# Feed-forward weights of blocks 3 to 14 loaded in pairs into the three buffers that later hold activations

## The chip, the core and the metric

The kernel runs on one core of a Trainium2 chip. The core has five engines with queues of their own: TensorE (PE, matrix products; its weight loads are shown as PEld), VectorE (DVE), ScalarE (ACT), GpSimd (POOL) and SyncE (SP). SP does no arithmetic here; it issues nearly all transfers between the chip's main memory (HBM) and the core's memory (SBUF). Each engine works through its own instructions in a fixed order and stops at one whose inputs or buffers are not ready; whatever stands behind it on that engine stops too. Matrix results land in PSUM, in banks that must be read out before they are used again.

The metric is device time in microseconds (us) of one execution.

## What is computed

One step of a model layer over 640 tokens (128 of a prompt, 512 of a sample) with a width of 1024: two mixers, an output projection with a layer norm, and then the feed-forward part, which is where the change lies. The last stage of the reference, cut to what matters:

```python
D_MODEL = 1024
D_FF = ((8 * D_MODEL // 3 + 255) // 256) * 256      # 2816

x = layer_norm(ALPHA * x + gate1 * mix, p['ln1_g'], p['ln1_b'])
h = x * (1.0 + scale2) + shift2
gt, up = jnp.split(h @ p['ffn_w_in'], 2, axis=-1)   # (1024, 2 * 2816)
ff = (jax.nn.silu(gt) * up) @ p['ffn_w_out']        # (2816, 1024)
x = layer_norm(ALPHA * x + gate2 * ff, p['ln2_g'], p['ln2_b'])
```

All of it is float32. The kernel gets float32 accuracy from a matrix unit that rounds its operands: it splits each operand into a high and a low part and sums three products (high x high, high x low, low x high).

## The kernel before

**Stages.** The program has a long first part (filters, the projections with `in_w_in`, the two mixers, `proj_a`, `proj_b`, `w_out`), up to about 970 us. Then comes the first half of the feed-forward part (`ffn_w_in`: gate and up projections, SiLU, product), up to 1267.8 us, and then the second half (`ffn_w_out`, the products named `fo`) to the end.

**The first half** walks over 22 blocks j of 128 feed-forward columns. Block 0 is done plainly. Blocks 1 to 21 use a Winograd-like scheme (class `Wino` with the name "f") that turns the gate and up products of a block into seven products of half the depth, numbered 1, 2, 4, 5, 6, 7 and 3; each is 12 matmuls of 128x320. Here `6_j` is short for product 6 of block j. They run into three PSUM banks per block (a: products 1, 6, 7, 4; b: 2; c: 5, 3), and after each product an ACT copy or a DVE operation (`post`, `ffn_done`) reads the bank before the next product adds to it. The tiles of these reads are `fc1`, `fu2`, `fu3` and `y`.

**Weights of a block.** Two loads of 512 KB, row 0 (gate columns, `rf0_j`) and row 1 (up columns, `rf1_j`), go into SBUF buffers with the tag "raw" (`Wino.raw`). There are `RAW_BUFS = 3` of these, so a block and a half. Then ACT rounds to the high part (`CAST`, names ending in h) and DVE subtracts for the low part (names ending in l): `wfg` from row 0 as loaded (products 1 and 2), `wfa` from half of row 1 (product 4), and, after three DVE additions and subtractions within the raw tiles, `wfs` (product 6), `wfu` (7 and 5), and after a fourth `wfv` (product 3). These split operands have 3 buffers (g, a, v) or 2 (s, u), so they can be made about two blocks before their products run. Both raw tiles of a block are free once its `wfu` and `wfv` parts are done. In the traces all these DVE operations stand under one line, that of the helper `tt`.

**What sets the order.** The program is written in periods (`PERIOD`): in period j stand the loads and splits of block j+1, then `6_j 2_j 1_(j+1) 4_(j-1) 5_j 7_j 3_(j-1)`. A scheduler then lays each engine's instructions out by its own estimate of when they can start, with priority for the bank reads. What it lays down is fixed; on the chip, an instruction that waits longer than estimated holds up its queue.

**Results.** The outputs of blocks 0 to 15 (`y_j`) are stored to HBM (`ad`), in the same SP queue as the loads. Those of blocks 16 to 21 stay in SBUF as `act8`, `act9` and `act10`: three buffers of 10,240 bytes per partition in the pool `arp`, opened at the end of `ffn_ops` and first written near 1210 us. The memory under this pool is that of the pool `lnr` (tiles `r` and `hf`, the normalised rows), which is closed just before, so that the first users of it wait for the last readers of `hf`.

Of the kernel before, what the change touches and what calls it, by code (L numbers as in the profile page):

```python
# [9 lines left out]
F32 = mybir.dt.float32  # L10
F32R = mybir.dt.float32r
# [6 lines left out]
P = 128  # L18
D = 1024
KT = 8  # L20
T = 640
# [109 lines left out]
FFN0 = "51 61 12 w2 71"  # L131
PERIOD = (("g", 1), ("w", 1), ("6", 0), ("2", 0), ("1", 1), ("4", -1), ("5", 0), ("7", 0), ("3", -1))
WPRI = 99
HIE = """SSSSVVSVSVSSSSSSSVVVSVVSVSSVSSSSSSSSSSSSSSSSSSSSSSSSSSSSSSSSSSSSSSSSSSSSSSSSSSSSSSSSSSSSSSSSSSSSSSSSSSSSSSSSSS"""
LOOK = """22222012202102201120122111222222222222222222222222222222222222222222222222222222222222222222222222222222222222"""
CONVSEQ = """a0 b0 c0 d0 e0 a1 b1 c1 f0 d1 e1 a2 b2 f1 s04 c2 s00 d2 x0 p0 s01 e2 i00 s02 a3 i01 s03 b3 i02 i03 f2 o00 c3 d3 e3 o01 a4 f3 s14 x1 s10 b4 c4 p1 s11 d4 i10 s12 e4 a5 i11 s13 b5 c5 d5 i12 f4 i13 o10 e5 a6 o11 f5 b6 s24 x2 s20 p2 s21 c6 i20 d6 s22 e6 i21 s23 a7 b7 i22 i23 c7 o20 f6 d7 o21 m0 e7 f7 s34 s30 n0 x3 m1 p3 s31 i30 s32 i31 s33 n1 i32 i33 o30 o31"""
# [26 lines left out]
def body(tc, I, O):  # L163
# [16 lines left out]
    def tt(out, a, b, op, eng=None):  # L180
        return (eng or V).tensor_tensor(out=out, in0=a, in1=b, op=op)  # L181
# [4 lines left out]
    def f32(ap):  # L186
        return ap.bitcast(F32)

    def pool(name, bufs=1, space=None, side=None):
        kw = dict(name=name, bufs=bufs, reuse_waits="tile")  # L190
        if space is not None:
            kw["space"] = space
        if side is not None:
            kw["side"] = side
        cm = tc.tile_pool(**kw)
        p = cm.__enter__()
        return p, (lambda: cm.__exit__(None, None, None))
# [6 lines left out]
    wp, close_wp = pool("wp")  # L204
# [132 lines left out]
    RAW_BUFS, HL_BUFS = 3, 3  # L337
    stream = dict(specs=[], hl=[], pos=0, stop=None)

    def w_fm(wap, col):  # L340
        return (wap.rearrange("(k p) n -> p k n", p=P)[:, :, col:col + P], (KT, P), None)
# [4 lines left out]
    def issue(i):  # L346
        src, (a, b), own = stream["specs"][i]
        raw = wp.tile([P, a, b], F32, tag="raw", bufs=RAW_BUFS, name=f"raw{i}")
        SY.dma_start(raw, src)
        if own is None:  # L350
            q, th, tl, n = wp, "wh", "wl", HL_BUFS
        else:
            q, th, tl, n = own[0]["p"], "wbh", "wbl", own[1]
        hi = q.tile([P, a, b], F32R, tag=th, bufs=n, name=f"wh{i}")
        lo = q.tile([P, a, b], F32R, tag=tl, bufs=n, name=f"wl{i}")
        with tc.high_priority():
            (V.tensor_copy if HIE[i] == "V" else S.copy)(hi, raw)  # L357
            tt(lo, raw, f32(hi), ALU.subtract, G if i < len(WSUB) and WSUB[i] == "G" else V)
        stream["hl"].append((hi, lo))
# [257 lines left out]
    def split(hl, at, src, eng="S"):  # L617
        h_, l_ = (x[(slice(None),) + at] for x in hl)
        (V.tensor_copy if eng == "V" else S.copy)(h_, src)
        tt(l_, src, f32(h_), ALU.subtract)  # L620


    class Wino:
# [5 lines left out]
            self.W, self.Y, self.B = {}, {}, {}  # L629

        def raw(self, j, row):
            t = wp.tile([P, KT, P], F32, tag="raw", bufs=RAW_BUFS, name=f"r{self.nm}{row}_{j}")
            SY.dma_start(t, w_fm(*self.cols(j)[row])[0])
            return t

# [887 lines left out]
    fn_ = {}  # L1523
# [52 lines left out]
    def plain_post(half):  # L1576
        g, u = (BK[x, half][:, 0:HT] for x in "gu")
        if half == 0:
            Y["y", 0] = fn_["p"].tile([P, T], F32, tag="y", bufs=3, name="y0")
            y = Y["y", 0][:, 0:HT]  # L1580
            act(y, g, AF.Silu)
            tt(y, u, y, ALU.mult)
        else:
            y1 = fn_["p"].tile([P, HT], F32, tag="u2", bufs=3, name="yp")
            act(y1, g, AF.Silu)
            half1(0, y1, u)

    def half1(j, y1, u):
        y = Y["y", j]
        tt(y[:, HT:HT + 64], y1[:, 256:HT], u[:, 256:HT], ALU.mult)  # L1590
        tt(y[:, HT + 64:T], y1[:, 0:256], u[:, 0:256], ALU.mult)
        if j < NSP:
            SY.dma_start(ad[j], y)
            return
        if j % 2 == 0:
            fn_["act", j // 2] = fn_["ar"].tile([P, 2, 2, T], F32R, name=f"act{j // 2}")
        t = fn_["act", j // 2]
        split((t[:, 0], t[:, 1]), (j % 2,), y)

# [6 lines left out]
    def ffn_done(n, j, ps):  # L1606
        Y = ffn.Y
        if n == 1:
            Y["c1", j] = ffn.keep("c1", 1, j, ps)
        elif n == 2:  # L1610
            Y["y", j] = fn_["p"].tile([P, T], F32, tag="y", bufs=3, name=f"y{j}")
            y = Y["y", j][:, 0:HT]
            tt(y, ps, Y["c1", j], ALU.add)
            act(y, y, AF.Silu)
        elif n == 6:
            Y["u2", j] = ffn.keep("u2", 3, j, ps)
        elif n == 7:
            u3 = ffn.keep("u3", 2, j, ps)
            tt(u3, ffn.B["c", j][:, 0:HT], u3, ALU.add)
            Y["u3", j] = u3  # L1620
        elif n == 4:
            y = Y["y", j][:, 0:HT]
            tt(y, ps, y, ALU.mult)
        elif n == 3:
            y1 = Y["u2", j]
            tt(y1, ps, y1, ALU.add)
            act(y1, y1, AF.Silu)
            half1(j, y1, Y["u3", j])

    ffn = Wino("f", lambda tag: fn_["p"], ffn_x, ffn_cols, ffn_done, WPRI)  # L1630
    W, Y, BK, ffn_run, prod_mm = ffn.W, ffn.Y, ffn.B, ffn.run, ffn.mm
# [154 lines left out]
```

## Time and profile before

| | us |
|---|---|
| median of 3 runs | 1429.8 (1427.77 to 1691.48) |
| the profiled execution | 1430.8 |
| its span in the profile | 1428.1 |
| first half of the feed-forward part, blocks 3 to 21 | about 1004 to 1267.8 |
| PE busy in the whole span | 1377.5 |

The span runs from the first to the last instruction; the 2.7 us between it and the execution's time lie around it. PE is busy nearly throughout, so what can be won is the time in which PE waits, and where matmuls follow one another closely a stretch is best read by their count: twelve back to back took 1.76 us. A row of the windows view gives, for a stretch of the span, its length, then the busy time of each engine with the count of instructions, the granted clock of PE, the busy share of the DMA engines and GB/s. In the rows of the timeline, what stands in brackets is the idle time of the engine before the row and what ended it.

### The profile page before, as it was taken

Reading aid. Unit: us, or ns where it says so; the run is one execution under the profiler, and the core shown is the slowest. Engines: PE = TensorE matmul, PEld = TensorE weight load, DVE = VectorE, ACT = ScalarE, POOL = GpSimd, SP = SyncE. Lnnn points to the kernel's source line nnn. Section 1 sums busy time; section 2 is a strip of 40 time slices with the busy share of each in tenths; the row PEclk is TensorE's granted clock in tenths of the full one; section 3 lists DMA queues with packets and bytes.
Section 4 is the critical chain, followed back from the end, with each engine's and each line's share of the span. In section 5 each row is a group of like instructions: output and inputs, shape, how many; then the busy total and the mean of one; then the engine's idle time right before and its main releaser. Section 6 shows DMA issues by size and latency. Waiting matters only on the chain. (4 is left out here: it accounts for less than half of the span.)

```text
span 1428.1 us, 23421 instructions
## 1 busy us (share of the span) xinstructions
PE 1377.5 (96%) x9513; PEld 1291.3 (90%) x9513; DVE 990.8 (69%) x1751; ACT 619.4 (43%) x1011; POOL 63.4 (4%) x56
## 2 busy tenths in 40 slices
PE   4989999999999999999999999998999999999997
PEld 2689889999999999999999999988999998998886
DVE  6886786647889734568778875578876766766427
ACT  3655554433323212455565673337444434442121
POOL 4230000020000000000000000000000000000003
PEclk9999999999999999999999999999999999999999
DMA  7944665674333374422232224632343233357211
GB/s 244 332 138 144 214 215 175 206 249 152 91 97 107 107 231 146 140 85 80 76 95 62 67 67 139 223 118 77 97 124 115 89 108 97 94 193 279 74 60 74
DMA packets 198855, 195.63 MB, mean 137 GB/s; under 512 B 7581, under 2 KB 155773, under 8 KB 197980
## 3 DMA queue, kind: packets, MB, share of 16 engines
q1 hardware_dynamic: 194860, 179.75, 40.0%
q0 software_dynamic: 2160, 9.15, 1.7%
q10 hardware_dynamic: 1728, 5.24, 0.9%
q8 instruction: 74, 1.21, 0.3%
q14 instruction: 33, 0.27, 0.1%
HBM read 162.91 MB, written 31.21 MB: 136 GB/s over the span
## 5 line engine op out<-in xcount | busy, mean ns | idle before, releaser
L181 DVE TENSOR_TENSOR wl<-raw,wh 128x1024 fp32r<-128x1024 f32 x96 | 117.2, 1223 | 134.1 <-ACT wh L357 133.4
L357 ACT CAST wh<-raw 128x1024 fp32r<-128x1024 f32 x90 | 94.1, 1049 | 221.1 <-PE pb L611 41.0
L1424 PE MATMUL fo<-wh,act 128*128 128x512 f32 (+1 forms) x440 | 130.6, 380 | 0.0
L1424 PEld LDWEIGHTS fo<-wh,act 128*128 128x128 f32 x440 | 81.2, 188 | 15.9
L1424 PE MATMUL fo<-wl,act 128*128 128x512 f32 (+1 forms) x220 | 83.4, 379 | 0.0
L611 PE MATMUL hy<-hTh,wh 128*128 128x320 f32 x256 | 79.6, 311 | 0.0
L611 PE MATMUL hy<-hTh,wl 128*128 128x320 f32 x256 | 79.1, 309 | 0.0
L611 PE MATMUL hy<-hTl,wh 128*128 128x320 f32 x256 | 79.1, 309 | 0.0
L611 PE MATMUL f<-hTh,wh 128*128 128x320 f32 x224 | 70.7, 316 | 0.0
L611 PE MATMUL f<-hTl,wh 128*128 128x320 f32 x224 | 69.6, 311 | 0.0
L611 PE MATMUL f<-hTh,wl 128*128 128x320 f32 x224 | 69.2, 309 | 0.0
L181 POOL TENSOR_TENSOR y<-y,gb 128x512 f32<-128x512 f32 x8 | 11.6, 1453 | 905.8 <-ACT y L170 905.5
L1424 PEld LDWEIGHTS fo<-wl,act 128*128 128x128 f32 x220 | 41.3, 188 | 7.9
L611 PEld LDWEIGHTS hy<-hTh,wh 128*128 128x128 f32 x256 | 48.1, 188 | 0.0
L611 PEld LDWEIGHTS hy<-hTl,wh 128*128 128x128 f32 x256 | 48.1, 188 | 0.0
L611 PEld LDWEIGHTS hy<-hTh,wl 128*128 128x128 f32 x256 | 48.0, 188 | 0.0
L170 ACT ACT_TABLE_LOAD x36 | 46.2, 1283 | 1.4 <-PEq L1770 0.7
L708 PE MATMUL v<-wh,hTl 128*128 128x256 f32 x160 | 45.1, 284 | 1.4 <-POOL hTl L181 1.4
L708 PE MATMUL v<-wl,hTh 128*128 128x256 f32 x160 | 44.8, 284 | 1.6 <-DVE wl L181 1.6
L708 PE MATMUL v<-wh,hTh 128*128 128x256 f32 x160 | 44.6, 283 | 0.0
L611 PEld LDWEIGHTS f<-hTl,wh 128*128 128x128 f32 x224 | 42.2, 188 | 0.0
L611 PEld LDWEIGHTS f<-hTh,wh 128*128 128x128 f32 x224 | 42.1, 188 | 0.0
(2291 smaller groups left out, 4699.1 us busy)
## 6 DMA issues: line engine op xcount, KB each, us to landing
raw<-in_w_in SPq DMA_DIRECT2D x52, 512.0 KB, 3.9
rf<-in_ffn_w_in SPq DMA_DIRECT2D x42, 512.0 KB, 4.9
araw<-in_ada_w SPq DMA_DIRECT2D x20, 1024.0 KB, 6.1
rm<-in_w_in SPq DMA_DIRECT2D x28, 512.0 KB, 4.8
raw<-in_ffn_w_out SPq DMA_DIRECT2D x22, 512.0 KB, 4.9
sd<-my SPq DMA_DIRECT2D x28, 320.0 KB, 2.3
kk<-kd SPq DMA_DIRECT2D x20, 256.0 KB, 2.6
ad<-y SPq DMA_DIRECT2D x16, 320.0 KB, 4.0
```

The costliest lines, as they stand in the source:

```text
L170: r = S.activation(out, in_, func, bias=bias, scale=scale)
L181: return (eng or V).tensor_tensor(out=out, in0=a, in1=b, op=op)
L357: (V.tensor_copy if HIE[i] == "V" else S.copy)(hi, raw)
L611: r = PE.matmul(ps[:, 0:HT], w[a][:, k, :], x[b][:, k, c0:c0 + HT], start=k == 0 and i == 0, stop=k == kt - 1 and i == 2)
L708: PE.matmul(ps[:, (t - t0) * 256:(t - t0) * 256 + 256], hT[b][:, k, t * P:t * P + P], w[a][:, k % 4, :], start=k == 0 and i == 0, stop=k = ...
L1424: PE.matmul(ps, x(t, b, k0 + kk), w[a][:, kk, :], start=first and kk == 0 and i == 0, stop=last and kk == nk - 1 and i == 2)
```

## The change

The raw weights of blocks 3 to 14 no longer go through the three "raw" buffers. Both rows of such a block go into one tile `rp{j}` of the pool `arp`, under the tag "act", which `act8` to `act10` now share. So there are three pair buffers for blocks 3 to 14 (twelve pairs, four turns), after which the same three buffers take the activations. The "raw" buffers, which blocks 3 to 14 leave alone, are next used by blocks 15 and up. The arithmetic is the same.

```diff
+FFN_PAIRS = range(3, 15)
...
         def raw(self, j, row):
-            t = wp.tile([P, KT, P], F32, tag="raw", bufs=RAW_BUFS, name=f"r{self.nm}{row}_{j}")
+            if self.nm == "f" and j in FFN_PAIRS:
+                if row == 0:
+                    pair = fn_["ar"].tile([P, 4 * T], F32, tag="act", bufs=3, name=f"rp{j}")
+                    self.W[j, "pair"] = pair[:, 0:2 * D].rearrange("p (r k n) -> p r k n", r=2, k=KT)
+                t = self.W[j, "pair"][:, row]
+            else:
+                t = wp.tile([P, KT, P], F32, tag="raw", bufs=RAW_BUFS, name=f"r{self.nm}{row}_{j}")
             SY.dma_start(t, w_fm(*self.cols(j)[row])[0])
             return t
...
-            fn_["act", j // 2] = fn_["ar"].tile([P, 2, 2, T], F32R, name=f"act{j // 2}")
+            fn_["act", j // 2] = fn_["ar"].tile([P, 2, 2, T], F32R, tag="act", bufs=3, name=f"act{j // 2}")
```

Since buffers come free at other times, the scheduler lays the instructions out differently from block 3 on. Three places show it. In each, `rf0_j` and `rf1_j` are the rows of block j in "raw" buffers and `rp{j}` is a pair (a load of it is one row of the pair).

SP's queue where block 3 begins, before:

```order
L1501 DMA xd_68<-r4_9803 128x1024
L633 DMA rf1_2_10604<-in_ffn_w_in 128x8x128
L633 DMA rf0_3_10641<-in_ffn_w_in 128x8x128
L1593 DMA ad_71<-y0_10438 128x640
L633 DMA rf1_3_10647<-in_ffn_w_in 128x8x128
L633 DMA rf0_4_10772<-in_ffn_w_in 128x8x128
L633 DMA rf1_4_10778<-in_ffn_w_in 128x8x128
L1593 DMA ad_71<-y1_10493 128x640
```

And in the changed kernel, at the same place:

```order
L1508 DMA xd_68<-r4_9803 128x1024
L640 DMA rf1_2_10604<-in_ffn_w_in 128x8x128
L640 DMA rf0_15_12201<-in_ffn_w_in 128x8x128
L1600 DMA ad_71<-y0_10438 128x640
L640 DMA rp3_10641<-in_ffn_w_in 128x8x128 x2
L640 DMA rp4_10771<-in_ffn_w_in 128x8x128 x2
L640 DMA rp5_10901<-in_ffn_w_in 128x8x128 x2
L640 DMA rf1_15_12207<-in_ffn_w_in 128x8x128
L640 DMA rf0_16_12332<-in_ffn_w_in 128x8x128
L1600 DMA ad_71<-y1_10493 128x640
```

Row 0 of block 15 takes the place of row 0 of block 3, three whole pairs follow the store of y0 together, and the rest of block 15 and a row of block 16 come right after them, about twelve blocks ahead of their use. The first row of `rp3` waits for the last reader of `hf`, the DVE operation `t4l<-hf1`.

ACT's queue where block 3 is split, before (`fc1`, `fu2`, `fu3` are the bank reads that PE's next products need):

```order
L677 COPY fu2_2_10681<-fa2_10589 128x320
L619 CAST wfa3h_10649<-rf1_3_10647 128x512
L619 CAST wfg4h_10774<-rf0_4_10772 128x1024
L677 COPY fu3_2_10752<-fa2_10589 128x320
L619 CAST wfs3h_10656<-rf0_3_10641 128x512
L619 CAST wfu3h_10660<-rf1_3_10647 128x1024
L619 CAST wfv3h_10665<-rf0_3_10641 128x512
```

And in the changed kernel:

```order
L620 CAST wfg3h_10643<-rp3_10641 128x1024
L620 CAST wfa3h_10648<-rp3_10641 128x512
L684 COPY fu2_2_10680<-fa2_10589 128x320
L620 CAST wfg4h_10773<-rp4_10771 128x1024
L620 CAST wfa4h_10778<-rp4_10771 128x512
L684 COPY fc1_3_10711<-fa3_10698 128x320
L620 CAST wfg5h_10903<-rp5_10901 128x1024
L620 CAST wfu3h_10659<-rp3_10641 128x1024
L684 COPY fu3_2_10751<-fa2_10589 128x320
L620 CAST wfs3h_10655<-rp3_10641 128x512
```

Casts of blocks 4 and 5 moved ahead of the cast `wfs3h`, which the first product of period 3 needs.

ACT's queue in a period in the middle, before (block 13 is split here; `fc1_12` reads product 1 of block 12, `fu3_11` product 7 of block 11):

```order
L170 ACTIVATE y11_11875<-y11_11875 128x320
L677 COPY fc1_12_11891<-fa12_11878 128x320
L619 CAST wfa13h_11959<-rf1_13_11957 128x512
L619 CAST wfg14h_12084<-rf0_14_12082 128x1024
L619 CAST wfu13h_11970<-rf1_13_11957 128x1024
L677 COPY fu3_11_11931<-fa11_11747 128x320
L619 CAST wfs13h_11966<-rf0_13_11951 128x512
L619 CAST wfv13h_11975<-rf0_13_11951 128x512
```

And in the changed kernel, at the same bank reads:

```order
L620 CAST wfg14h_12073<-rp14_12071 128x1024
L171 ACTIVATE y11_11865<-y11_11865 128x320
L684 COPY fc1_12_11881<-fa12_11868 128x320
L620 CAST wfa13h_11948<-rp13_11941 128x512
L620 CAST wfs13h_11955<-rp13_11941 128x512
L684 COPY fu3_11_11921<-fa11_11738 128x320
L620 CAST wfu13h_11959<-rp13_11941 128x1024
L620 CAST wfv13h_11964<-rp13_11941 128x512
```

Between `fc1_12` and the bank read `fu3_11` there stood three casts, of row 1 of block 13 and of row 0 of block 14, all from "raw" buffers; now two stand there, and `wfg14h` and `wfu13h` have moved to places ahead of `fc1_12` and behind `fu3_11`. All of them read pairs. From the split of block 16 on, each queue stands as it did before. SP then issues the store of y11, row 1 of block 16, the store of y12, row 0 of block 17, row 1 of block 17, and so on.

## The prediction

> **What bounds the kernel now.** I read the busy shares and the chain of waits first:
>
> ```profile
> PE 1377.5 (96%) x9513; PEld 1291.3 (90%) x9513; DVE 990.8 (69%) x1751; ACT 619.4 (43%) x1011; POOL 63.4 (4%) x56
> PE fo L1424 10%; DMA rf<-in_ffn_w_in 6%; PE pa L611 4%; PE wo L1424 4%; DVE rf L181 2%; PE fa L668 1%; PE mga L611 1%; PE fc L668 1%; DVE fu L181 1%; DVE y L181 1%; PE fg L1573 1%; PE fo_last L1424 1%; PE fb L668 0%; PE fu L1573 0%; DMA raw<-in_ffn_w_out 0%
> ```
>
> PE is at 96%, so at most some 50 us can be won anywhere. The chain's largest part that isn't PE is the load that the change moves, 6% of 1428, about 86 us. That isn't the gain: PE works beside it. What PE loses is read from the stage. The windows, cut where product 4 of blocks 3, 8 and 19 begins:
>
> ```profile
> 1035.90:1097.40 61.50, 61.50 (x422) 61.50 (x421) 45.59 (x74) 28.36 (x50) 0.00 (x0) 1.00 0.38 115
> 1097.40:1245.80 148.40, 140.01 (x927) 135.37 (x926) 99.50 (x167) 63.81 (x112) 0.00 (x0) 1.00 0.33 99
> 1267.80:1416.00 148.20, 148.20 (x704) 124.35 (x703) 73.89 (x106) 36.40 (x45) 9.04 (x6) 1.00 0.40 140
> ```
>
> Five blocks took 61.5 us, 12.3 each, with PE and its loads full. The next eleven took 148.4 us, 13.49 each: 148.4 - 11 x 12.3 = 13.1 us lost. After that PE is full to the tail, and DVE (half busy) and ACT are not the limit anywhere: a microsecond won in these blocks reaches the end. Who PE waits for in the second window:
>
> ```profile
> PEld fc L668 <- DVE fu L181: 8.1, 11, 1.9
> PEld fa L668 <- ACT fu L677: 5.0, 7, 1.6
> ```
>
> 8.1 + 5.0 = 13.1 us, the same loss. Step by step, with one wait more behind the window:
>
> ```profile
> L668 PE MATMUL fa<-t4h,wfa8h x4: 306/308/309, 1097.4 to 1098.7; 128*128 128x320 f32 x4
> L668 PE MATMUL fa<-t4h,wfa14h x4: 306/308/309, 1177.8 to 1179.1; 128*128 128x320 f32 x4
> L668 PE MATMUL fa<-t4h,wfa16h x4: 309/309/412, 1204.7 to 1206.1; 128*128 128x320 f32 x4
> L668 PE MATMUL fa<-t4h,wfa19h x4: 306/308/309, 1245.8 to 1247.1; 128*128 128x320 f32 x4
> 1248.22 0.19 PEld L668 LDWEIGHTS fc<-xxh,wfu20h 128*128 128x128 f32 x1 [0.78 <-DVE fu L181]
> ```
>
> From product 4 of block 8 to that of block 14 (six steps) 6.6 us are lost, from there to block 16 2.3, to block 19 4.2, and 0.8 at block 20. These are waits for bank reads, not for weights. Why the reads are late shows in one of them, on ACT, PE's weight loads and DVE:
>
> ```profile
> 1129.80 0.41 ACT L677 COPY fc<-fa 128x320 f32<-128x320 f32 x1
> 1132.75 0.62 ACT L619 CAST wfa13h<-rf 128x512 fp32r<-128x512 f32 x1 [2.54 <-DMA rf<-in_ffn_w_in]
> 1135.18 1.05 ACT L619 CAST wfg14h<-rf 128x1024 fp32r<-128x1024 f32 x1 [1.81 <-DMA rf<-in_ffn_w_in]
> 1136.14 1.04 ACT L619 CAST wfu13h<-rf 128x1024 fp32r<-128x1024 f32 x1
> 1137.08 0.41 ACT L677 COPY fu<-fa 128x320 f32<-128x320 f32 x1
> 1137.55 0.19 PEld L668 LDWEIGHTS fa<-t4h,wfa11h 128*128 128x128 f32 x1 [0.76 <-ACT fu L677]
> 1133.40 0.69 DVE L181 TENSOR_TENSOR wfa13l<-rf,wfa13h 128x512 fp32r<-128x512 f32 x1 [3.62 <-ACT wfa13h L619]
> 1138.74 0.88 DVE L181 TENSOR_TENSOR fu<-fc,fu 128x320 f32<-128x320 f32 x2
> ```
>
> ACT stood 2.54 and 1.81 us at casts whose weights had not landed; the copy `fu3_11` stood behind them, and PE's product 4 of block 11 behind the copy. DVE stood 3.62 us the same way, with the reads of bank c behind it. So the loss is a load's delay, passed on by two in-order queues. Why the load is late, from the chain in order of time:
>
> ```profile
> 1102.08 5.82 DMA rf<-in_ffn_w_in
> 1107.91 1.06 ACT wfg12h L619
> 1109.00 1.23 DVE wfg12l L181
> 1110.22 0.61 DVE rf L181
> 1110.86 0.69 DVE rf L181
> 1111.55 0.80 DVE fu L181 x2
> 1113.45 1.13 DVE wfu11l L181
> 1114.58 0.61 DVE wfv11l L181
> 1115.25 5.87 DMA rf<-in_ffn_w_in
> ```
>
> A closed loop: the last split of block 11 frees the buffers, two rows are loaded, and the next split starts when they land. One turn is 13.2 us here (1102.08 to 1115.25), and the load is 5.8 of it.
>
> **The change part by part.**
>
> *It takes the load out of the loop for blocks 3 to 14.* Each pair buffer is reloaded three blocks before it is needed. When the split of block j ends, the pair for j+3 goes out and has two blocks, 24.6 us, for some 6 us of loading. SP's stores of y between the rows of later pairs wait for blocks finished earlier than that. So ACT and DVE find their weights there, and what paces the splits is PE itself (the two buffers of `wfs` and `wfu`). The loss of the eleven blocks falls to whatever comes back after block 14.
>
> *What comes back.* From the split of block 16 on the loop is the old one, at about 13.7 us a turn: nine turns lie between the first and the last of
>
> ```profile
> 1101.39 0.61 DVE wfv10l L181
> 1224.49 0.61 DVE wfv19l L181
> ```
>
> or (1224.49 - 1101.39) / 9. Against PE's 12.3 the splits fall back by 1.4 us a block. How far back they may fall:
>
> ```profile
> L181 DVE TENSOR_TENSOR wfv9l<-rf,wfv9h x1: 693/693/693, 1088.1 to 1088.1; 128x512 fp32r<-128x512 f32 x1
> L668 PE MATMUL fa<-t4h,wfa7h x4: 306/308/309, 1085.1 to 1086.4; 128*128 128x320 f32 x4
> DMA to landing us min/median/max: 3.9/4.9/5.9
> ```
>
> Split 9 ended at 1088.8, 3.7 us after product 4 of block 7 began; that is about where the first small waits appear, so I take +3.7 as the limit. In the new kernel split 15 is paced by PE and ends about 2.3 us after period 13's last product (`wfu` 1.1, a bank read 0.5, `wfv` 0.6). Its row 1 buffer is free at 1.3 and the next at 3.0 (behind the store of y12). Adding the landing of 4.9, the cast 1.06, `wfg` low part 1.23 and two operations (1.3) gives 11.5; then the bank reads wait for PE until 13.0, and `wfs`, `wfu`, y and `wfv` end split 16 at 16.0. Product 4 of block 14 starts at 12.3 + 5.3 = 17.6 on this clock (5.3 is three products of 1.76), so split 16 stands at -1.6, and 17 to 21 at -0.2, 1.2, 2.6, 4.0 and 5.4. Only the last two pass 3.7, by 0.3 and 1.7. I keep 1.0 us, with 0 and 5.0 as ends (5.0 is what was lost after block 16: 4.2 + 0.8).
>
> *The entry.* Pairs lie where `hf` lay. They wait for its last reader, and three pairs come at once:
>
> ```profile
> L181 DVE TENSOR_TENSOR t4l<-hf,t4h x3: 424/682/682, 1000.9 to 1003.0; 128x512 fp32r<-128x512 f32 x2, 128x256 fp32r<-128x256 f32 x1
> 1022.00:1024.00 2.00, 2.00 (x16) 2.00 (x15) 0.07 (x1) 0.73 (x2) 0.00 (x0) 1.00 1.01 339
> 1017.24 0.19 PEld L668 LDWEIGHTS fa<-t2h,wfs3h 128*128 128x128 f32 x1 [0.35 <-ACT wfs3h L619]
> 1017.98 0.19 PEld L668 LDWEIGHTS fa<-t2h,wfs3l 128*128 128x128 f32 x1 [0.30 <-DVE wfs3l L181]
> 1030.86 0.19 PEld L668 LDWEIGHTS fa<-t2h,wfs4l 128*128 128x128 f32 x1 [0.72 <-DVE wfs4l L181]
> ```
>
> The first row leaves at 1003.0 + 0.7 = 1003.7 and lands after 3.9 to 4.9, at about 1008. That is in time: PE has twenty matmuls of blocks 1 and 2 before product 1 of block 3, which the scheduler has moved back to about 1009.5. At full rate (339 GB/s) a row takes 1.6 us, and 2.0 by the difference of 5.9 and 3.9. So `rp5`'s first row, the fifth, lands 6.4 to 8.0 us after the first, at 1014.1 to 1016.0. ACT's queue has `wfg5h` ahead of `wfs3h`: with 1.05 + 1.05 + 0.42 + 0.62 behind it (`wfg5h`, `wfu3h`, a copy, `wfs3h`) `wfs3h` is there at 1017.2 to 1019.1. PE wants it at 1017.1, so 0.1 to 2.0 us are lost, and perhaps 0.5 on its low part. I take 1.5 against the 0.65 now lost there.
>
> The burst can be weighed by the Trainium skill, DMA: Bandwidth & Descriptors, section Bandwidth, which has 1 MB in 6.15 us (341 GB/s) as the rate of one large transfer. The best row here, 339 GB/s, agrees. By that rate alone the fifth row would be there at 1013, the stall at `wfs3h` would be nought, and the sum 1.5 us lower.
>
> *The rest costs nothing:* the same loads, casts and products are issued, in other places. The early rows of blocks 15 and 16 come behind the pairs. `act8` takes a pair buffer that is free after the split of block 12, some 40 us before its first write. The pair views have the same shapes as the raw tiles. If that cover were gone, a late `act8` would cost its one split, under 2 us.
>
> **The sum.** Lost before: 13.1, 0.8 at block 20, 0.65 at block 3 and 0.72 at block 4, together 15.3. Lost after: 1.5 at the entry, 1.0 at the end, and 1.0 for waits that the new order may hold. 15.3 - 3.5 = 11.8 us. 1430.8 - 11.8 = 1419.0. The median of the runs lies 1.0 us under the profiled execution, so against it the gain would read as 10.8.
>
> **Rivals.**
>
> *The loop takes the lead back.* If split 16 starts its turn later than I worked out (landing 5.9, not 4.9, a store of y ahead), the waits of blocks 17 to 20 come back. Then 5.0 stands in place of 1.0 at the end: 15.3 - 7.5 = 7.8, or 1423.0. For it: the queues stand in the old order from there on. Against it: the first five blocks of the old kernel lost nothing with the same loop. The Trainium skill, Perfetto Trace Analysis, section Optimization Strategy, says that a bubble which repeats can mean too few buffers for the next tile; by that rule it comes back wherever there are three buffers, which is this rival.
>
> *Nothing moves.* The bank reads stay late because the casts now wait for PE to release split buffers, and the reads stand behind these as they stood behind loads: about 1430. Against it: in the new order a cast waits for a product that PE runs before the one whose read stands behind.
>
> *Slower.* The same mechanism, but each period loses more than before: if a cast held by PE holds ACT for the 2.1 us which one did before,
>
> ```profile
> ACT wfa8h L619 <- PE fc L668: 2.1, 1, 2.1
> ```
>
> twelve blocks lose 25 us; with 6.6 of the old loss gone (the steps to block 14), 1430.8 + 25.2 - 6.6 = 1449.4. It decides once a period loses over 0.55 us (6.6 / 12). Against it: PE lost nothing at that place.
>
> **How the numbers follow.** My forecast has a chance of 0.71 (1414 to 1422), the loop's return 0.14 (1423), nothing moved 0.08, slower 0.07. So 1414 to 1428 takes in the first two and leaves out 0.15 and a little at the lower end; its lower bound is both stalls at nought (the 1.5 and the 1.0) and 2.5 of spread between runs. Two per cent, about what a measurement of this kernel can tell from no change, is 28.6 us: more than PE loses in the whole stage. Faster by that much would need a second gain that I don't see (0.01), slower by it more than my slow rival (0.02); the rest, 0.97, is within.
>
> **What would show it.** Right: the eleven steps of product 4 from block 8 to 19 at 12.3 us each; no load ends an idle time of ACT in blocks 5 to 14; the waits of `fc` and `fa` gone there; the first pair landing by 1008.6. The loop is back if the waits reappear from block 17. Wrong: casts that wait for PE with bank reads behind them, or a stall of several microseconds at `wfs3h`.

## The result, and the profile after

| | before | after |
|---|---|---|
| median of 4 runs each, us | 1428.78 | 1415.52 |
| the same without the run of 1691.48 us, us | 1427.77 | 1415.52 |
| the profiled execution, us | 1430.8 | 1414.7 |
| its span in the profile, us | 1428.1 | 1412.6 |

The ratio is 0.9913, with a 95% interval from 0.9896 to 0.9930 (one run of before, of 1691.48 us, was disturbed and is left out of it). By the medians without that run the change saves 12.25 us: faster beyond the interval, and inside the 2% up to which the forecast counted a time as the same. The page of the changed kernel gives the busy time of each engine and the chain that ended last:

```profile
PE 1371.9 (97%) x9513; PEld 1291.7 (91%) x9513; DVE 995.5 (70%) x1751; ACT 620.8 (44%) x1011; POOL 63.4 (4%) x56
PE fo L1431 10%; PE fa L675 10%; PE fc L675 5%; PE pa L612 4%; PE wo L1431 4%; PE fb L675 2%; PE mga L612 1%; PE fg L1580 1%; PE fo_last L1431 1%; DMA rp<-in_ffn_w_in 1%; PE fu L1580 0%; PE xh L1500 0%; ACT hf L171 0%; PE u L1269 0%; SPq L640 0%; PE sc L1249 0%
```

The load of feed-forward weights, which made up 6% of the chain before, is at 1% (`rp`), and the products of the feed-forward blocks (`fa`, `fc`, `fb`) stand in its place: the chain now runs through PE. The two windows that answer to those of before, cut again where product 4 of blocks 3, 8 and 19 begins, and product 4 of blocks 14 and 19:

```profile
1033.90:1095.30 61.40, 61.40 (x421) 61.40 (x421) 48.52 (x78) 29.34 (x53) 0.00 (x0) 1.00 0.40 120
1095.30:1230.60 135.30, 135.30 (x927) 135.30 (x926) 97.27 (x158) 60.42 (x106) 0.00 (x0) 1.00 0.27 82
L675 PE MATMUL fa<-t4h,wfa14h x4: 306/308/309, 1169.1 to 1170.4; 128*128 128x320 f32 x4
L675 PE MATMUL fa<-t4h,wfa19h x4: 306/308/309, 1230.6 to 1231.9; 128*128 128x320 f32 x4
```

Eleven blocks take 135.3 us, 12.3 each, with PE and its weight loads full; before it was 148.4. All weight-load waits between 975 and 1260 us that the waits view still lists (engine and tile, what it waited for, total us, times, longest):

```profile
PEld fg L1580 <- ACT b12h L620: 3.4, 1, 3.4
PEld fc L675 <- ACT xxh L620: 0.7, 1, 0.7
PEld fa L675 <- ACT wfs3h L620: 0.3, 1, 0.3
PEld fa L675 <- ACT wfs2h L620: 0.2, 1, 0.2
PEld fa L675 <- DVE wfs3l L182: 0.2, 1, 0.2
```

The first two lie ahead of block 3 and were the same before. The other three, 0.7 us, are what is left of the 15.3 in the changed stage. ACT's queue over the split of block 13, in the changed kernel's timeline (in brackets the idle time ahead of the row and what ended it):

```profile
1118.23 1.05 ACT L620 CAST wfg14h<-rp 128x1024 fp32r<-128x1024 f32 x1 [0.84 <-PE fb L675]
...
1120.19 0.43 ACT L684 COPY fc<-fa 128x320 f32<-128x320 f32 x1 [0.54 <-PE fa L675]
1121.74 0.62 ACT L620 CAST wfa13h<-rp 128x512 fp32r<-128x512 f32 x1 [1.13 <-PE fa L675]
1125.30 0.62 ACT L620 CAST wfs13h<-rp 128x512 fp32r<-128x512 f32 x1 [2.93 <-DVE rp L182]
1125.83 0.42 ACT L684 COPY fu<-fa 128x320 f32<-128x320 f32 x1
1126.14 1.05 ACT L620 CAST wfu13h<-rp 128x1024 fp32r<-128x1024 f32 x1
```

None of these rows waits for a load. Two casts wait for PE to release their buffers (0.84 and 1.13 us) and `wfs13h` waits 2.93 us for DVE, none of which costs PE anything. Where the rows come through raw buffers again, ACT still waits for loads, 1.0 to 2.8 us at each `wfg` and `wfa` of blocks 17 to 21, and that costs PE nothing either.

One more reading is needed to compare executions. The program's head, which no version touches, doesn't take the same time in each: the first matmul of `wo` began at 914.8 us in the execution of before, at 913.6 in that of after, and between 913.6 and 918.5 over all executions below. So below each profile is read from the first matmul of `wo` to the start of the last of `fo` with `wl`, a stretch called "wo to fo". The rows of before and of after, from each kernel's view of these tiles:

```profile
L1424 PE MATMUL wo<-wh,mixh x80: 389/392/483, 914.8 to 972.1; 128*128 128x512 f32 x80
L1424 PE MATMUL fo<-wl,act x220: 279/389/398, 1268.1 to 1415.8; 128*128 128x512 f32 x99, 128*128 128x256 f32 x11
```

```profile
L1431 PE MATMUL wo<-wh,mixh x80: 387/392/479, 913.6 to 970.8; 128*128 128x512 f32 x80
L1431 PE MATMUL fo<-wl,act x220: 279/389/398, 1252.2 to 1399.9; 128*128 128x512 f32 x99, 128*128 128x256 f32 x11
```

1415.8 - 914.8 = 501.0 us before, 1399.9 - 913.6 = 486.3 us after: the change is worth 14.7 us by this measure. The profiled executions differ by 16.1; 1.2 of that came from the head.

### The profile page after: what moved, and what is told of

Read it like the earlier page. It is cut to its first block, busy times and chain, and to the rows that moved or that the text cites. A ratio compares the mean times of both kernels' runs of the same rounds, so it can differ in the third digit from the quotient of the medians.

```text
span 1412.6 us, 23432 instructions
## 1 busy us (share of the span) xinstructions
PE 1371.9 (97%) x9513; PEld 1291.7 (91%) x9513; DVE 995.5 (70%) x1751; ACT 620.8 (44%) x1011; POOL 63.4 (4%) x56
```

## Experiments

The theory: splits and loads stood in a closed loop that was slower than PE; the pairs take the load out of it for blocks 3 to 14, and the lead that this builds lasts to the end. The rivals that the runs are to tell apart: the gain comes from the order in which the scheduler now lays out ACT and DVE; or it comes from the pairing of the rows; or PE waits because bank reads stand behind casts, whatever the loop's rate. Times are single runs except in the row with a ratio, where 4 runs stand against 7 of before. On the chips of these runs the kernel before took 1431.0 to 1433.6 us. Since the heads differ, the wo to fo column decides.

| run | edit | time, us | wo to fo, us |
|---|---|---|---|
| before | | 1430.8 | 501.0 |
| after | pairs for 3 to 14 | 1414.7 | 486.3 |
| e1 | pairs for 3 to 8 | 1426.8 | 496.8 |
| e2 | pairs for 3 to 11 | 1422.3 | 489.0 |
| e3 | pairs for 3 to 20 | 1416.9 | 486.3 |
| e10 | pairs for even blocks only | 1418.4 | 488.7 |
| e6 | only row 1 in the large buffers | 1416.9 | 486.4 |
| e9 | pairs, with the old order | 1414.1 | 486.3 |
| e5 | after, row 0 of 6 to 14 loaded twice | 1416.1 | 486.2 |
| e7 | before, bank reads ahead of casts | 1428.9 | 499.2 |
| e4 | before, row 0 of 6 to 14 loaded twice | 1423.5 | 492.5 |
| e13 | e4 with the old order on ACT and DVE | 1449.5 | 518.0 |
| e11 | before, in the order `wfs`, bank read, `wfu`, then `wfg` of the next block | 1419.0 (ratio 0.9915, 0.9899 to 0.9932) | 489.1 |

### How long the lead lasts: e1, e2, e3

```diff
-FFN_PAIRS = range(3, 15)
+FFN_PAIRS = range(3, 9)      # e1
+FFN_PAIRS = range(3, 12)     # e2
+FFN_PAIRS = range(3, 21)     # e3
```

> Only blocks 3 to 8 go through pairs; 9 to 21 use the raw buffers again. Theory (the pairs take the load out of the loop and so build up a lead, which the loop then eats at about 1.4 us a block): in the changed kernel the split of the first block after the pairs ended 2.7 us before the product 4 two blocks back began, and each later one about 1.4 us nearer. So here splits 9 to 13 cost PE nothing, the limit (about +5) is reached at split 14, and then some six blocks lose 1.2 us each: 7 us, about 1422.5 us, with the step from product 4 of block 8 to that of block 14 (73.8 us at full rate) at most 2 us too long and the whole loss after it. Rival (no lead: a block loses as soon as it is back in the raw buffers): every block from 9 on loses 1.2 us, some 13 us, about 1428 us.

> Blocks 3 to 11 go through pairs, 12 to 21 through the raw buffers. With pairs to block 8 PE lost 10.5 us more than with pairs to block 14; losses began six blocks behind the last pair, at about 1.4 us a block. Theory (the lead lasts about six blocks): the first loss at product 4 of block 16, and some 4 to 6 us in all, 490 to 492.5 us from the first matmul of wo to the last of fo. Rival (loss goes with the number of blocks left in the raw buffers, 10.5 us for six of them): 1.75 us each for three, 491.5 us too, but with the loss beginning right behind block 11.

> Blocks 3 to 20 go through pairs (the last of them share the three buffers with the activations that are written then). Theory (nothing is left to win in the late blocks, since the lead lasted to the end in the changed kernel): 1415.5 us, within 1; the loads that ACT waited for at blocks 17 to 19 are there in time, and PE gains nothing by it. Rival (the forecast's term for the late blocks was right and something of 1 to 5 us still stands there): 1 to 5 us faster than the changed kernel.

The steps of product 4 from block to block, worked out from its first starts in each trace, are 12.3 us up to block 12 in e1 and up to block 15 in e2: four blocks after the last pair PE still loses nothing. (The weights of two blocks further on are being split then, so it is the seventh split behind the last pair that first costs something.) Then e1 has 12.6, 12.8, 14.8, 13.1, 15.1, 13.2 and 13.2 for the steps to blocks 13 to 19, and e2 has 12.7, 12.8, 13.0 and 12.9 for those to blocks 16 to 19. In e1 the waits view (1030 to 1260 us) has the two old waits again and nothing else:

```profile
PEld fc L675 <- DVE fu L182: 6.5, 7, 1.9
PEld fa L675 <- ACT fu L684: 3.0, 5, 0.8
```

The first loss in e2 is where it was expected. So the lead is real, and the loop takes it back as soon as the pairs end. The sizes were off: 10.5 us lost in e1 against 7 expected (by its sum alone e1 is nearer to the rival's 13), 2.7 in e2 against 4 to 6. What decides against the rival without a lead is where the loss begins, in both. In e3 two blocks run in another order (steps of 10.5 and 14.1 to blocks 17 and 18), the sum of the two steps is the same, and wo to fo is 486.3, as in after; the whole time, 1416.9, is 0.4 above what was expected, with a head 1.6 us longer. The late blocks of the changed kernel have nothing left to give.

### The order with the new buffers: e9

```diff
+                order_after(C["g", j][0], C["a", j - 1][0])
+                order_after(C["u", j - 1][0], C["g", j][0])
+                order_after(C["u3", j - 3], C["u", j - 1][0])
+                order_after(C["s", j - 1][0], C["u3", j - 3])
+                order_after(C["u", j - 1][1], C["s", j - 1][1])
```

(for j from 6 to 15; `C` holds the cast and the subtraction of each split and the bank copies; `order_after` lays the first behind the second in its queue.)

> The changed kernel with its pair buffers, but ACT and DVE are made to issue the casts, subtractions and bank reads of blocks 5 to 14 in the order of the kernel before: wfa, wfg of the next block, wfu, then the bank read fu3, then wfs and wfv. Theory (the loads, not the order, made the reads late): the casts find their weights in SBUF, so the reads behind them come in time: 1415.5 to 1417.5 us. Rival (the gain comes from the order in which the scheduler now lays the queues, with one cast fewer ahead of fu3): 10 to 13 us come back, 1426 to 1429 us, with the waits of fc and fa at product 4 and 3 as before.

It took 486.3 us from wo to fo, the same as after; the whole time, 1414.1, is even below the 1415.5 to 1417.5 expected. Its ACT timeline at block 13:

```profile
1121.84 0.62 ACT L620 CAST wfa13h<-rp 128x512 fp32r<-128x512 f32 x1 [1.13 <-PE fa L682]
1122.36 1.05 ACT L620 CAST wfg14h<-rp 128x1024 fp32r<-128x1024 f32 x1
1125.73 1.05 ACT L620 CAST wfu13h<-rp 128x1024 fp32r<-128x1024 f32 x1 [2.32 <-DVE rp L182]
1126.69 0.42 ACT L691 COPY fu<-fa 128x320 f32<-128x320 f32 x1
1127.01 0.62 ACT L620 CAST wfs13h<-rp 128x512 fp32r<-128x512 f32 x1
```

These are the casts of before in the order of before, with the same bank read behind three of them; where ACT stood 2.54 and 1.81 us for loads, it now waits 1.13 us for PE and none for `wfg14h` (`wfu13h` waits 2.32 us for DVE instead). With the pairs the old order costs nothing.

### How much memory, and does pairing matter: e6, e10

```diff
-            if self.nm == "f" and j in FFN_PAIRS:        # e6: row 1 alone, one row in each large buffer
+            if self.nm == "f" and j in FFN_PAIRS and row == 1:
...
-FFN_PAIRS = range(3, 15)                                 # e10
+FFN_PAIRS = range(4, 16, 2)
```

> Of blocks 3 to 14 only row 1 goes into the three large buffers, one row in each; row 0 goes into the raw buffers. So each row of a block has three buffers, as with the pairs, but nothing is paired, and the first rows 0 needn't wait for the last reader of hf. Theory (the number of blocks that can be on their way counts): 486 to 488 us from the first matmul of wo to the last of fo, all products 4 from block 3 to 19 at 12.3 us a step. Rival (it matters that a block's two rows come together, or that row 0 leaves the raw buffers): the waits of fc and fa return, 5 us or more.

> Only the even blocks 4 to 14 go through pairs; the odd ones use the raw buffers, so six blocks in place of twelve are moved. Theory (what counts is that a block's rows can be issued more than a period ahead; with half of the blocks out of them the three raw buffers hold one and a half of every two blocks): the loads of the odd blocks are out of the loop as well, at most 2 us of the gain are lost: 1415 to 1418 us. Rival (each moved block wins its own 1.1 us): half of the gain, about 1422 us.

e6 took 486.4 us, with all sixteen steps of product 4 from block 3 to 19 at 12.2 or 12.3: pairing doesn't matter; three buffers for each of the two rows are enough. e10 has the same steps and took 488.7, 2.4 more than after, where at most 2 were expected. 2.1 of them are lost ahead of product 4 of block 3, where the waits view has 2.0 us at `wfs3h` (0.3 in after): row 1 of block 3 stands behind four rows of pairs in SP's queue. Six blocks out of the raw buffers are as good as twelve, as the theory has it; the rival, a gain for each moved block, falls.

### More load: e5 and e4, and a surprise

```diff
-            SY.dma_start(t, w_fm(*self.cols(j)[row])[0])
+            for _ in range(2 if self.nm == "f" and 6 <= j < 15 and row == 0 else 1):
+                SY.dma_start(t, w_fm(*self.cols(j)[row])[0])
```

> The changed kernel with the same addition: row 0 of blocks 6 to 14 is loaded twice, one load after the other into its pair. Theory (pairs are reloaded two blocks, 24.6 us, before they are needed, so that the load is in no loop): the same addition costs 0 to 2 us, 486.3 to 488.3 us from the first matmul of wo to the last of fo. Rival (the changed kernel is in a loop of the same kind and has only a little to spare): 10 us or more are lost.

> The kernel before; row 0 of blocks 6 to 14 is loaded twice, one load after the other into the same buffer. From the first matmul of wo to the last of fo the kernel before took 501.0 us, the changed one 486.3. Theory (in the kernel before, the load is part of a closed loop): each of nine turns grows by one more landing behind the other, 3 to 5 us, and PE loses nearly all of it: 27 to 45 us longer than before, some 528 to 546 us. Rival (transfers are hidden beside PE; order or something else made the waits): within 3 us of before.

e5 took 486.2 us: nine rows more cost the changed kernel nothing. e4 is a plain miss, of the rival too: the same nine rows made the kernel before faster, 492.5 us against 501.0, with all steps of product 4 up to block 16 at 12.3. The chain of e4 (start, us, what) and its ACT timeline show how:

```profile
1113.21 4.42 DMA rf<-in_ffn_w_in
1117.65 3.82 DMA rf<-in_ffn_w_in
```

```profile
1119.41 1.05 ACT L619 CAST wfu12h<-rf 128x1024 fp32r<-128x1024 f32 x1
1121.50 1.05 ACT L619 CAST wfg13h<-rf 128x1024 fp32r<-128x1024 f32 x1 [1.04 <-DMA rf<-in_ffn_w_in]
...
1141.21 1.05 ACT L619 CAST wfg15h<-rf 128x1024 fp32r<-128x1024 f32 x1 [1.81 <-DMA rf<-in_ffn_w_in]
...
1144.15 1.05 ACT L619 CAST wfu14h<-rf 128x1024 fp32r<-128x1024 f32 x1 [1.57 <-DVE rf L181]
```

Both landings of row 0 of block 13 are there, 8.2 us, but only `wfg13h` waits for them, and in e4 `wfg13h` stands behind `wfu12h`. A turn was 11.5 us (its splits 10 to 12 ended at 1100.9, 1112.3 and 1123.8). Row 0 of block 15 is loaded once, and there `wfg15h` stands ahead of `wfu14h` as in before; from split 14 on the turns are 13.2 to 14.9 us, and PE loses 5.6 us from block 17 on. So my picture of the loop had a gap: what stands in it depends on the order of the splits. Two runs follow from that.

### The order with the old buffers: e11, e13, e7

```diff
+                order_after(C["u3", j - 3], C["s", j - 1][0])      # e11, j from 6 to 21
+                order_after(C["u", j - 1][0], C["u3", j - 3])
+                order_after(C["g", j][0], C["u", j - 1][0])
+                order_after(C["v", j - 1][0], C["g", j][0])
+                order_after(C["g", j][1], C["v", j - 1][1])
```

> The kernel before with its three raw buffers, every row loaded once; from block 5 on ACT issues wfa, wfs, the bank read fu3, wfu, and only then wfg of the next block and wfv (DVE likewise), the order in which the run with row 0 loaded twice had turned out. Theory, revised after that run (the loop is as long as it is because wfg of the next block stands ahead of wfu, so that both loads must land within a turn; behind wfu, row 0 lands beside the split): a turn of 11.5 us or less, under PE's 12.3, no waits of fc and fa, 486.5 to 489 us from the first matmul of wo to the last of fo, as fast as the changed kernel without a new buffer. Rival (the old buffers limit the rate in any order, and the doubled load helped in another way): 13.2 us a turn or more, 497 to 502 us.

It came out at 489.1 us, at a ratio to before (0.9915) that can't be told from that of the changed kernel (0.9913). All steps from block 5 to 19 are 12.2 or 12.3, and while the splits caught up (8 to 12) a turn took 10.7 to 11.7 us. Of the 2.8 us that it lacks to 486.3, 2.1 are waits of `fa` at product 4 of blocks 3 and 4, where the old order meets the new one. ACT at block 13, and PE from 1100 to 1235 us in the windows view:

```profile
1126.33 0.62 ACT L619 CAST wfa13h<-rf 128x512 fp32r<-128x512 f32 x1 [1.13 <-PE fa L675]
1129.88 0.62 ACT L619 CAST wfs13h<-rf 128x512 fp32r<-128x512 f32 x1 [2.93 <-DVE rf L181]
1130.41 0.42 ACT L684 COPY fu<-fa 128x320 f32<-128x320 f32 x1
1130.73 1.05 ACT L619 CAST wfu13h<-rf 128x1024 fp32r<-128x1024 f32 x1
1131.68 1.04 ACT L619 CAST wfg14h<-rf 128x1024 fp32r<-128x1024 f32 x1
1100.00:1235.00 135.00, 135.00 (x924) 135.00 (x923) 104.74 (x170) 64.89 (x114) 0.00 (x0) 1.00 0.38 112
```

`wfg14h` finds row 0 of block 14 landed, since it stands 5 us behind `wfa13h` and not right behind it, and none of these casts waits for a load. Three raw buffers suffice if the split of a block doesn't stand behind the next block's row. (e11 moves `wfs` and the bank read ahead of `wfu` as well; no run moves `wfg` alone.)

> The kernel before with row 0 of blocks 6 to 14 loaded twice, as once already, but ACT is made to keep wfg of the next block ahead of wfu. Theory (with wfg ahead of wfu the load of row 0 is in the loop): each of the nine turns grows by a landing, 3 to 5 us; 27 to 45 us more than before, 528 to 546 us from the first matmul of wo to the last of fo. Rival (a load of row 0 is hidden whatever the order): within 5 us of before's 501.0.

e13 forces the order of before on e4, with the lines of e9 and three more like them. It lost 17.0 us against before: the direction expected, the size not. The chain has both landings, and behind them `wfg` ahead of `wfu`:

```profile
1098.32 5.41 DMA rf<-in_ffn_w_in
1103.75 3.80 DMA rf<-in_ffn_w_in
...
1107.57 1.04 ACT wfg10h L619
1108.62 0.95 ACT wfu9h L619
```

```profile
1048.20:1171.70 123.50, 108.83 (x677) 104.56 (x677) 75.95 (x122) 44.51 (x81) 0.00 (x0) 0.94 0.41 124
```

The windows row is that of the eight steps of product 4 from block 3 to 11: 15.4 us each against 12.3. The granted clock was 0.94 there, the chain of this turn passes through PE as well (3.4 us of `fa` from 1109.94), and the blocks behind it came out in an order that lost nothing, so the size isn't a clean measure of a landing.

```diff
-            split(hl, (), raw)
+            at = {"g": j - 3, "a": j - 2}.get(nm)                # e7, for wfg and wfa
+            behind = (None, None)
+            if self.nm == "f" and at is not None:
+                behind = (self.Y.get(("read7", at)), self.Y.get(("read3", at - 1)))
+            split(hl, (), raw, behind=behind)
...
```

(`read7` and `read3` are the bank reads after products 7 and 3; `split` lays the cast behind the first and the subtraction behind the second.)

> The kernel before with its raw buffers, but the bank reads fu3 (ACT) and that of product 3 (DVE) are put ahead of the casts wfa, wfg and their subtractions, which wait for loads. Theory (the loop of split and load is a limit of its own, at 13.3 to 13.7 us a turn; the order only decides which instruction PE is seen to wait for): at most 3 us of the 14.7 are won, 498 to 505 us from the first matmul of wo to the last of fo. Rival (the order is the cause: late loads hurt only because reads stand behind them): most of the loss goes without any new buffer, 486 to 491 us.

e7 won 1.8 of the 14.7 us. A row of its waits view (eight more blocks have one like it), and then a turn of its chain (start, us, what):

```profile
PEld fa L672 <- DVE wfs14l L181: 1.0, 1, 1.0
```

```profile
1105.97 4.79 DMA rf<-in_ffn_w_in
1110.79 1.06 ACT wfg12h L619
1111.87 1.22 DVE wfg12l L181
...
1114.92 1.06 ACT wfu11h L619
...
1118.84 0.60 DVE wfv11l L181
...
1119.46 4.57 DMA rf<-in_ffn_w_in
```

With the bank reads out of the way PE waits for the split operands themselves, and loses nearly as much: a turn is 13.5 us (1105.97 to 1119.46), and PE isn't in it. `wfg12h` still stands ahead of `wfu11h`. So it isn't the reads behind the casts that cost most of the time. They were only where a loop slower than PE first showed.

## Why the prediction was right, and where not

**The time.** 1419.0 was forecast, within 1414 to 1428; the median is 1415.5. The gain was forecast at 11.8 against the profiled execution and measured at 14.7 from wo to fo; the difference is losses that I kept and that weren't there. The 12.25 us of the medians are nearer to the forecast by chance: the profiled execution of before lies 3.0 us above 1427.77 (the forecast's 1.0 rests on a median that took in the run of 1691.48), that of after 0.8 below 1415.52.

**What PE loses and where (15.3 us).** Right. 15.3 - 0.7 = 14.6 of the 14.7 are the waits that the prediction listed.

**The pairs take the load out of the loop.** Right, and shown both ways: e5 loads nine more rows and loses nothing, e1 and e2 end the pairs early and get the old waits back. At `wfa` of blocks 7 to 16 ACT waits for PE instead of for loads (1.1 us each), which was the start of the slow rival; PE lost nothing by it. One sign named in the forecast didn't hold: loads still end idle times of ACT at `wfg5h` to `wfg7h` (0.81, 1.69 and 1.12 us), in the burst at the entry, without cost to PE.

**Why the loop was slow.** Here the prediction was incomplete. It called the loss "a load's delay, passed on by two in-order queues". e7 shows that the passing on by the bank reads is worth 1.8 us of 14.7, and e4 and e11 show what the step left out: the loop is that long only in the order of before. The turn shown in the forecast has a landing and then the 2.3 us of `wfg12` (1.06 + 1.23) ahead of `wfu11`. That the place of `wfg` is what matters fits e4, e7, e11 and e13, but no run moves it alone, so this part is argued. The change takes the load out of the loop; another order gets the loop below PE's 12.3 us as well.

**What comes back after block 14 (1.0 kept).** The places were right to 1.3 us, the limit wasn't. Forecast for the ends of splits 16 to 21 against product 4 two blocks back: -1.6, -0.2, 1.2, 2.6, 4.0, 5.4. Measured: -0.6, 0.8, 2.1, 3.9, 4.4, 4.5. The row for 21 in after, whose product 4 (block 19) stands above, and the first wait of the old kernel's late order:

```profile
L182 DVE TENSOR_TENSOR wfv21l<-rf,wfv21h x1: 683/683/683, 1234.4 to 1234.4; 128x512 fp32r<-128x512 f32 x1
1099.24 0.19 PEld L668 LDWEIGHTS fc<-xxh,wfu9h 128*128 128x128 f32 x1 [0.18 <-DVE fu L181]
```

1234.4 + 0.7 - 1230.6 = 4.5, and PE waits nowhere; so +3.7 was too low a limit. The forecast read it from split 9 of the old kernel, but the first wait there (0.18 us at 1099.24) falls into the making of split 10, which ended at 1102.0, 4.6 us after product 4 of block 8 began. The other runs agree: first waits come while the split is made that ends at +4.9 in e1 (split 15), at +5.0 in e2 (18), at +4.8 in e10 and +4.6 in e6 (both 21). This holds for that order only: splits 5 to 7 of the old kernel, in another order, ended at 5.9 to 6.5 and PE lost nothing.

**The entry (1.5 kept).** Mis-sized; measured 0.5 to 0.7 us of waits. ACT and one weight load of PE there:

```profile
1009.51 1.05 ACT L620 CAST wfg4h<-rp 128x1024 fp32r<-128x1024 f32 x1 [0.71 <-DMA rp<-in_ffn_w_in]
1011.37 0.62 ACT L620 CAST wfa4h<-rp 128x512 fp32r<-128x512 f32 x1 [0.81 <-DMA rp<-in_ffn_w_in]
1013.12 1.05 ACT L620 CAST wfg5h<-rp 128x1024 fp32r<-128x1024 f32 x1 [0.81 <-DMA rp<-in_ffn_w_in]
1015.34 0.62 ACT L620 CAST wfs3h<-rp 128x512 fp32r<-128x512 f32 x1
1016.01 0.19 PEld L675 LDWEIGHTS fa<-t2h,wfs3h 128*128 128x128 f32 x1 [0.33 <-ACT wfs3h L620]
```

Casts of `rp4` and `rp5` that wait for their rows start 1.8 us apart, between the 1.6 and 2.0 that bounded the term, and the stall at `wfs3h` is 0.33, near the lower of its ends (0.1 and 2.0). The Trainium skill, DMA: Bandwidth & Descriptors, section Bandwidth, has 341 GB/s for 1 MB, measured with transfers that GpSimd issues; 512 KB every 1.8 us is about 290 GB/s, so this burst ran slower than that. By that rate the fifth row would come an estimated 6.2 us after the first (1013.8 by the working of the forecast, which says 1013); it came 7.0 us or somewhat more after it, at 1013.12 against 1006.16 or earlier, which fits the forecast's 6.4 to 8.0.

**Waits of the new order (1.0 kept).** Nought: after has none, and e9 with the old order has none either.

**The rival that too few buffers would bring the waits back.** The Trainium skill, Perfetto Trace Analysis, section Optimization Strategy, has that a repeating bubble can mean too little memory for the next tile. e1 agrees: with the raw buffers back, the waits are back. e11 doesn't: the same three raw buffers in another order have none from block 5 to 19. The measurement decides: here it was buffers or order, either one.

## What to carry to other kernels

When one engine waits a little in every period, find the loop that feeds it, with every landing and instruction in one turn, and compare its turn with the engine's period: the instruction that is seen to be waited for may be only where it shows. Such a loop is broken by buffers that let the load go out earlier, or by moving out of it whatever the next step doesn't need; the second costs no memory. A lead, once built up, hides a slower loop until it is used up, so a change need not cover the whole stage. Here the splits ended 2.7 us ahead of product 4 of two blocks back with pairs, fell back by about 1.3 us each without them, and cost nothing until they ended about 4.6 us behind it: some six splits, in e1 and e2 alike.

## What the runs showed that I had not expected

The head of the program, the same in all versions, took from 913.6 to 918.5 us up to the first matmul of `wo` in the thirteen profiled executions, a spread of 4.9 us against a gain of 14.7. Only a stretch of the trace that begins behind it shows differences of a microsecond.

A kernel given more to load became faster (e4, 8.5 us): the scheduler, given two loads of row 0 to place, laid the queue in a better order.
